# Modulation in half-width pieces of all row blocks from free tiles, and local attention with negated scores and the sink as a column

## The chip, the cores and the metric

The kernel runs on one core of a Trainium2 chip. The metric is device time in microseconds of one execution; a kernel's time is the median of its runs. The engines are TensorE (PE, its weight loads shown as PEld), VectorE (DVE), ScalarE (ACT), GpSimd (POOL) and SyncE (SP), which issues the kernel's DMAs.

## What is computed

Two layers of a diffusion backbone over 512 latent and 256 context tokens, model width 1024, in float32. Each layer is modulated by a projection of the conditioning, runs three attention branches beside each other and merges them:

```python
for l in range(DEPTH):
    mod_lat = silu_c @ w_mod[l] + b_mod[l]      # 1024 -> 3 * 1024: shift, scale, gate
    mod_ctx = silu_cc @ w_mod[l] + b_mod[l]
    ...
    x, ctx = hybrid_layer(x, ctx, mod_lat, mod_ctx, ..., l < DEPTH - 1)
return rms_norm(x, final_norm)

# one layer, cut
h_lat = rms_norm(x, norm_g) * (1.0 + scale) + shift
... = split_cols(h_lat @ w_in)                  # latent, differential and local attention, z, g
x = x + gate * merge_branches((ya_l, yb_l, yc_l), z_l, gm_l, w_branch, w_out)

# local attention: a window of 128 tokens on either side, all context tokens, and a sink logit per head
s_loc = where(mask, q @ k.T, NEG_INF);  s_ctx = q @ k_ctx.T        # q scaled by 64 ** -0.5
p = softmax(concatenate([sink, s_ctx, s_loc]));  o = p_ctx @ v_ctx + p_loc @ v_loc
```

The sink takes part in the maximum and in the sum of the softmax and has no value row.

## The kernel before

The program is written out ahead of time by a planner in Python (`Plan`), which keeps a clock of its own for each engine and for the DMA queue and puts the next piece that is ready by this clock into each engine's order. On the chip each engine then runs its order and waits on semaphores; where the planner's clock was wrong, an engine stands still at the head of its order. Two streams give PE its work. Stream A (`stream_a`) is attention: scores, then transposes and products with the values, for units of two rows of 128 queries, local attention first, then differential, then latent attention. Stream B (`stream_b`) is a list of entries: the projections in the order of `SEQ`, then the merges of the three branches in the order of `BR`, local attention's first, then the output projection. An entry may ask for a number of free tiles (`need`, with a reserve `keep`) and stands until they are there. Beside the streams, single pieces may be spawned with `P.pe`; a piece that is ready by the planner's clock goes ahead of both streams.

Weights come through `weight_stream`: SP loads each item of 512 KB into one of two buffers `ws`, ACT writes its high half into a tile `wh` and DVE its low half, and PE multiplies three passes (high-high, high-low, low-high). A `ws` buffer is free again when its item is `staged`, that is split; an item with `split=False` keeps its buffer until its entry has run. All other loads and stores also go through SP's one queue, in the planner's order. Activations live in 46 tiles of 128 x 768 (`slot`, `free`, `room`).

The modulation is a product of `sil` (the conditioning of both token groups, in 32 columns) with `w_mod`, a chunk `n` of 512 columns at a time, eight row blocks `kt` of 128. Block `kt` writes the 32 partitions of strip `kt % 4` of one bank, so two blocks add up in each strip, and `mod_fin` adds the four strips with another product. Chunks 0 to 3 of layer 0 are worked in the setup (`mod_load`, `mod_now`, not changed). Chunks 4 and 5 of layer 0 (its gate) and all six chunks of layer 1 are entries of stream B (`mod_entry`): four entries for each chunk, each with two row blocks of 512 columns as one unsplit item of the weight stream. Layer 0's eight stand ahead of its merges; layer 1's 24 follow one at a time after each `z` and `g` entry and every odd `b` entry of layer 0's merges (`some_mod`), until the list is empty. The planner charges a DMA 620 ns on SP's queue, then 650 ns, one ns for 350 bytes, and 1050 ns to land (`dma_t`).

Local attention's softmax (`soft_sink`, line 849) has for each row of 128 queries: one DVE scan that reads the scores from PSUM, adds the mask (0 or -1e30), writes them to a tile and takes the maximum, beginning with the sink (L858); a sign flip on DVE (L861); Exp of the sink on ACT into a column of its own; Exp of the scores on ACT with their sum; the sum of both on DVE; the reciprocal (L865); and the scaling by it, on DVE or ACT as the planner has it. There are 96 such rows in layer 0 and 64 in layer 1. L309, L323, L325, L330, L341 and L444 are helpers (ACT, DVE and POOL operations, the DMA and the matmul), so groups are told apart by their tiles; L579 is the modulation's matmul.

Of the kernel before, what the change touches and what calls it, by code (L numbers as in the profile page):

```python
# [18 lines left out]
AF = mybir.ActivationFunctionType  # L19
# [33 lines left out]
def shape_tables():  # L53

    pos = np.arange(LT)
    row, col = (pos // 64).astype(np.float32), (pos % 64).astype(np.float32)

    def ang(nf):
        inv = np.float32(10000.0) ** (-np.arange(nf, dtype=np.float32) / np.float32(nf))
        inv = inv.astype(np.float32)  # L60
        return np.concatenate([row[:, None] * inv, col[:, None] * inv], axis=1).astype(np.float32)

    a = ang(16).T
    p = np.arange(128)
    hd = a[p % 32]
    sgn = np.where(p % 64 < 32, -1.0, 1.0)[:, None]
    m = ang(8).T[p % 16]
    tab = np.concatenate([np.cos(hd), np.sin(hd) * sgn, np.cos(m), np.sin(m)], axis=1).astype(np.float32)
    ks = (np.sin(ang(8).T[np.arange(32) % 16]) * np.where(np.arange(32) < 16, -1.0, 1.0)[:, None])
    i, j = np.arange(128)[:, None], np.arange(128)[None, :]  # L70
    below = np.where(j >= i, 0.0, -1e30)
    above = np.where(j <= i, 0.0, -1e30)
    z = np.zeros((128, 128))
    mask = np.concatenate([below, z, above, z, z, below, z, z, z], axis=1)
    sel = np.zeros((128, 2))
    for g in range(4):
        sel[32 * g, 0] = sel[32 * g + 1, 1] = 1.0
    f = np.float32
    return {"tab": tab, "ktab": ks.astype(f), "mask": mask.astype(f), "sel": sel.astype(f)}
# [156 lines left out]
def hybrid_kernel(tc, x_in, c_in, ctx_in, c_ctx, w_mod, b_mod, norm_g, w_in, q_norm, w_uq, kv_norm, w_ukv,  # L236
# [52 lines left out]
    def tiny(n=1):  # L289
        return sb.tile([128, n], F32, name=nm("ti"), tag=f"ti{n}", bufs=24)  # L290
# [8 lines left out]
    def act(ready, out, in_, func=AF.Copy, scale=1.0, bias=None, accum=None, psum=True):  # L299
        kw = {}  # L300
        if accum is not None:
            kw["accum_out"] = accum
        if bias is not None:
            kw["bias"] = bias
        cost = 0.83 * fsz(out) + (51 if psum else 93) + (93 if accum is not None else 0)
        if not isinstance(scale, float) or bias is not None:
            cost += 93
        t = yield from P.on("A", ready, cost,
                            lambda: nc.scalar.activation(out=out, in_=in_, func=func, scale=scale, **kw))  # L309
        return t  # L310

    def dve(ready, emit, n, fast=False, ptr=False):
        t = yield from P.on("V", ready, (0.52 if fast else 1.04) * n + 70 + (60 if ptr else 0), emit)
        return t
# [25 lines left out]
    def dma(out, in_):  # L340
        nc.sync.dma_start(out=out, in_=in_)  # L341
        n = 4
        for s in out.shape:
            n *= s
        return dma_t(n)
# [39 lines left out]
    def item(load, parts=None, split=True, size=1024):  # L385

        done = When()
        return dict(load=load, parts=parts, split=split, size=size, ready=When(), done=done, staged=When() if split else done)
# [111 lines left out]
    def columns(st, n, t, out):  # L500
        o = {}

        def emit():
            o["p"], o["r"] = bk.take()
            nc.tensor.transpose(out=o["p"][:, 0:n], in_=st[0:n, 0:128], identity=ident[0:n, 0:n])
        t = yield from P.pe(lambda: max(t, bk.gate()), 110.0, emit)
        t = yield from dve(t, lambda: nc.vector.tensor_copy(out, o["p"][:, 0:n]), n)
        o["r"].t = t
        return t
# [35 lines left out]
    def setup2():  # L545

        st, v, pr = slot(), slot(), slot()
        n, t = rows_of(st, (q_norm[0], kv_norm[0], subln[0], b_mod[1], norm_g[1], q_norm[1], kv_norm[1], subln[1]))
        tv = 0.0
        for i, a in enumerate((lq1, lk1, lq2, lk2)):  # L550
            tv = max(tv, dma(v[:, i * 128:(i + 1) * 128], a.rearrange("l d -> (l d)").partition_broadcast(128)))
        dma(sinkt, sink.rearrange("l h -> (l h)").partition_broadcast(128))
        dma(rope, tab[:, 0:2 * LT].rearrange("p (a n) -> p a n", a=2))

        def chain():
            tcol = yield from columns(st, n, t, cols[:, 32:32 + n])
            vv = v[:, 0:512].rearrange("p (a l d) -> p a l d", a=4, l=2)
            prv = pr[:, 0:256].rearrange("p (m l d) -> p m l d", m=2, l=2)
            ta = tv
            for m in range(2):  # L560
                ta = yield from tt(ta, prv[:, m], vv[:, 2 * m], vv[:, 2 * m + 1], ALU.mult)
            d4, e4 = tiny(4), tiny(4)
            ta = yield from dve(ta, lambda: nc.vector.tensor_reduce(out=d4, in_=pr[:, 0:256].rearrange("p (a d) -> p a d", a=4), axis=AX.X, op=ALU.add), 256)
            ta = yield from act(ta, e4, d4, func=AF.Exp, psum=False)
            ta = yield from tt(ta, lamt, e4[:, 0:2], e4[:, 2:4], ALU.subtract)
            for l in range(2):
                li = 0.8 - 0.6 * math.exp(-0.3 * l)
                o = l * NCOL
                for t0, dst, src, k, op in ((ta, lamt[:, l:l + 1], lamt[:, l:l + 1], li, ALU.add),
                                            (tcol, subc[:, l:l + 1], cols[:, o + COL_SUB:o + COL_SUB + 1], li - 1.0, ALU.mult),  # L570
                                            (tcol, qnc[:, l], cols[:, o + COL_QN:o + COL_QN + 3], 96.0 ** -0.5, ALU.mult)):
                    yield from dve(t0, lambda: nc.vector.tensor_scalar(out=dst, in0=src, scalar1=k, scalar2=None, op0=op), 3)
            free(3)
        P.spawn(chain())


    def mod_mm(pm, kt, wv):
        g = kt % 4
        nc.tensor.matmul(pm[32 * g:32 * g + 32, :], lhsT=sil[:, kt], rhs=wv, start=kt < 4, stop=kt >= 4)  # L579

    def mod_fin(l, n, pm, rel, t):

# [264 lines left out]
        row["t"].t = t  # L847

    def soft_sink(u, row, p, rel, t):
        lo, hi = u["span"]  # L850
        n = hi - lo
        mx, nmx, s, e, r = tiny(), tiny(), tiny(), tiny(), tiny()
        sk = sinkt[:, u["l"] * 16 + row["h"]:u["l"] * 16 + row["h"] + 1]
        yield room(1)
        pt_ = slot()
        row["P"] = pt_
        mk = u["mask"]()
        t = yield from dve(t, lambda: nc.vector.tensor_tensor_reduce(  # L858
            out=pt_[:, 0:n], in0=p[:, lo:hi], in1=mk, scale=1.0, scalar=sk, op0=ALU.add, op1=ALU.max, accum_out=mx), n, ptr=True)
        rel.t = t  # L860
        t = yield from dve(t, lambda: nc.vector.tensor_scalar(out=nmx, in0=mx, scalar1=-1.0, scalar2=None, op0=ALU.mult), 1)  # L861
        t1 = yield from act(t, e, sk, func=AF.Exp, bias=nmx, psum=False)
        t = yield from act(t1, pt_[:, 0:n], pt_[:, 0:n], func=AF.Exp, bias=nmx, accum=s, psum=False)
        t = yield from tt(t, r, s, e, ALU.add)
        t = yield from dve(t, lambda: nc.vector.reciprocal(out=r, in_=r), 8)  # L865
        t = yield from normalise(t, pt_[:, 0:n], r)
        row["t"].t = t

# [417 lines left out]
    def build_layer(o):  # L1286
# [249 lines left out]
        def sec_sw():  # L1536
# [31 lines left out]
                    P.spawn(chain())  # L1568
            entry(sv_h, sv_its, need=6, keep=KEEP_SV)
            for pr in range(8):  # L1570
                qk_entry("sq", pr, C_SQ, 0.125, cx)
                if pr == 2:
                    qk_entry("sk", 1, C_SK, 1.0, True)

# [39 lines left out]
        m = [None] * 8  # L1614
        mH, mL, mt_ = [None] * 8, [None] * 8, [When() for _ in range(8)]
        o.m = {"HL": [mH, mL], "t": mt_}
        mod_left = [(n, j) for n in (2, 3, 0, 1, 4, 5) for j in range(4)]
        pm = {}

        def mod_entry(ll, n, j):  # L1620
            it = item(lambda t: [(t[:, 0:1024].rearrange("p (k c) -> p k c", k=2),
                                  w_mod[ll, j * 256:(j + 1) * 256, n * 512:(n + 1) * 512].rearrange("(k p) c -> p k c", p=128))], split=False)

            def h(it):
                yield lambda: max(at(it["ready"]), bk.gate() if j == 0 else 0.0)
                if j == 0:
                    pm["p"], pm["r"] = bk.take()
                for k in range(2):
                    mod_mm(pm["p"], 2 * j + k, it["ws"][:, k * 512:(k + 1) * 512])
                P.tick(550.0)  # L1630
                if j == 3:
                    P.spawn(mod_fin(ll, n, pm["p"], pm["r"], P.now + 200.0))
            entry(h, [it], need=0)

        def some_mod(k):
            for _ in range(k):
# [3 lines left out]
        if l == 0:  # L1640

            for n in (4, 5):
                for j in range(4):
                    mod_entry(0, n, j)

        def wide(it, X):
# [278 lines left out]
```

## Time and profile before

| | us |
|---|---|
| median of 3 runs | 2752.4 |
| lowest and highest run | 2744.74, 2753.49 |
| the profiled execution | 2746.83 |
| its span, first to last instruction | 2745.0 |
| PE busy in it | 2657.7 |
| DVE busy | 1655.3 |
| ACT busy | 1380.5 |
| POOL busy | 127.8 |
| mean granted clock of TensorE | 0.988 |

Times in the trace are microseconds from the span's start. A busy time is the union of an engine's instructions; matmuls are pipelined and their ends are modelled, so one matmul's record overlaps the next, and what a piece costs PE is read from its start to the start of the work after it. A value in square brackets in a timeline is the time that the engine stood idle ahead of the instruction, with what released it.

### The profile page before, as it was taken

The page shows a single profiled execution, that of the slowest core. Times are in us where ns is not written, and L with a number is a line of the kernel's source. Part 1 is how long each engine was busy: PE and PEld are TensorE (multiplying, and loading weights), DVE is VectorE, ACT ScalarE, POOL GpSimd, SP SyncE. Part 2 cuts the span into 40 slices and gives each one's busy share as a digit, 9 for nine tenths or more (in the row PEclk, how much of TensorE's full clock was granted, in tenths as well). Part 3 has the DMA queues.
Part 4 walks back from the last instruction along what each step waited for, and adds up shares of the span by engine and source line. Part 5 has one row for each costly group of instructions (what it writes and reads, how often), then busy time and mean ns, then how long its engine had stood idle before and what let it go on. Part 6 is the DMA issues. An engine that isn't in the chain of part 4 may idle for free.

```text
span 2745.0 us, 42932 instructions
## 1 busy us (share of the span) xinstructions
PE 2657.7 (97%) x16711; PEld 2308.7 (84%) x16711; DVE 1655.3 (60%) x3350; ACT 1380.5 (50%) x2860; POOL 127.8 (5%) x198
## 2 busy tenths in 40 slices
PE   7999999999999999999999999999999999999998
PEld 4888898888888878878888988898888789888888
DVE  4678778666676652133333578888767677634435
ACT  4667777555556442121222357877546555523332
POOL 0000000111100000000000000000011100000000
PEclk8999999999999999999999999999999999999999
DMA  6132211111122353353332443322112223443433
GB/s 228 45 92 83 73 42 46 49 51 48 44 68 87 107 187 105 93 175 93 91 86 62 139 125 92 105 57 67 40 48 55 58 68 102 127 136 110 123 101 130
DMA packets 328348, 249.58 MB, mean 91 GB/s; under 512 B 24548, under 2 KB 288320, under 8 KB 328144
## 3 DMA queue, kind: packets, MB, share of 16 engines
q1 hardware_dynamic: 328144, 246.83, 30.9%
q8 instruction: 131, 2.15, 0.3%
q14 instruction: 73, 0.60, 0.1%
HBM read 211.37 MB, written 35.41 MB: 90 GB/s over the span
## 4 chain that ended last, share of the span: by engine, by line
PE 78%; DVE 9%; ACT 7%; issue 3%; DMA 2%; POOL 1%; SPq 0%; DVEq 0%; ACTq 0%; POOLq 0%
PE wd L444 37%; PE bk L444 35%; PE bk L913 4%; ACT pt L309 3%; ACT s L309 3%; DVE pt L323 2%; DVE s L323 2%; PE bk L579 1%; DVE wh L323 1%; DVE s L858 1%; DVE s L330 1%; ACT wh L309 1%; DMA ws<-in_w_in_dram 1%; DVE ti L825 0%; POOL pt L325 0%
## 5 line engine op out<-in xcount | busy, mean ns | idle before, releaser
L444 PE MATMUL wd<-s,wh 128*128 128x512 f32 (+1 forms) x4392 | 855.5, 355 | 6.7 <-ACT wh L309 3.5
L444 PEld LDWEIGHTS wd<-s,wh 128*128 128x128 f32 x4392 | 725.7, 189 | 145.0 <-ACT s L309 12.9
L444 PE MATMUL bk<-s,wh 128*128 128x512 f32 (+1 forms) x3666 | 771.7, 356 | 18.4 <-DVE s L323 6.9
L444 PEld LDWEIGHTS bk<-s,wh 128*128 128x128 f32 x3666 | 582.5, 190 | 106.6 <-DVE s L323 9.8
L323 DVE TENSOR_TENSOR wh<-ws,wh 128x1024 fp32r<-128x1024 f32 (+4 forms) x294 | 325.1, 1112 | 343.1 <-ACT wh L309 341.4
L309 ACT ACTIVATE wh<-ws 128x1024 fp32r<-128x1024 f32 (+4 forms) x294 | 282.5, 967 | 297.1 <-PE wd L444 148.5
L309 ACT ACTIVATE pt<-bk 128x512 fp32r<-128x512 f32 (+3 forms) x604 | 341.4, 584 | 167.9 <-PE bk L913 102.8
L444 PE MATMUL bk<-wh,s 128*128 128x256 f32 x2688 | 352.9, 286 | 3.8 <-DVE wh L323 2.0
L444 PEld LDWEIGHTS bk<-wh,s 128*128 128x128 f32 x2688 | 333.3, 193 | 9.7 <-issue 3.2
L323 DVE TENSOR_TENSOR pt<-bk,pt 128x512 fp32r<-128x512 f32 (+3 forms) x400 | 257.6, 664 | 77.7 <-ACT pt L309 66.4
L444 PE MATMUL bk<-pt,s 128*128 128x256 f32 x1888 | 277.2, 288 | 13.3 <-DVE pt L323 10.2
L444 PEld LDWEIGHTS bk<-pt,s 128*128 128x128 f32 x1888 | 252.2, 191 | 38.8 <-DVE pt L323 16.7
L444 PE MATMUL wd<-s,s 128*128 128x256 f32 (+5 forms) x1872 | 275.9, 333 | 5.9 <-ACT s L309 5.5
L309 ACT ACTIVATE s<-wd,ti 128x768 f32<-128x768 f32 (+1 forms) x240 | 195.5, 818 | 140.8 <-DVE ti L825 78.5
L444 PEld LDWEIGHTS wd<-s,s 64*128 64x128 f32 (+2 forms) x1872 | 214.3, 191 | 36.7 <-ACT s L309 9.9
L913 PE MATMUL bk<-ident,s 128*128 128x128 f32 x1472 | 208.5, 275 | 9.8 <-DVE pt L323 2.4
L913 PEld LDWEIGHTS bk<-ident,s 128*128 128x128 f32 x1472 | 170.3, 142 | 35.9 <-ACT s L309 5.5
L309 ACT ACTIVATE s<-s,ti 128x512 f32<-128x512 f32 (+3 forms) x249 | 174.1, 708 | 15.0 <-DVE ti L865 8.1
L309 ACT ACTIVATE s<-bk 128x256 fp32r<-128x256 f32 (+5 forms) x291 | 113.6, 424 | 87.0 <-PE bk L444 85.0
L330 DVE SCALAR_TENSOR_TENSOR s<-s,wd 128x768 f32<-128x768 f32 (+1 forms) x58 | 47.6, 820 | 180.8 <-PE wd L444 108.1
L309 ACT ACTIVATE s<-wd 128x768 f32<-128x768 f32 (+1 forms) x58 | 40.9, 705 | 218.8 <-PE wd L444 218.8
L825 DVE TENSOR_REDUCE ti<-wd 128x1 f32<-128x768 f32 (+1 forms) x160 | 128.7, 843 | 18.2 <-PE wd L444 17.9
(98 smaller groups left out, 1734.6 us busy)
## 6 DMA issues: line engine op xcount, KB each, us to landing
ws<-in_w_in_dram SPq DMA_DIRECT2D x180, 512.0 KB
ws<-in_w_branch_dram SPq DMA_DIRECT2D x48, 512.0 KB
ws<-in_w_mod_dram SPq DMA_DIRECT2D x32, 512.0 KB
ws<-in_w_out_dram SPq DMA_DIRECT2D x24, 512.0 KB
y<-yo SPq DMA_DIRECT2D x80, 128.0 KB
s<-y SPq DMA_DIRECT2D x24, 384.0 KB
s<-s SPq DMA_DIRECT2D x22, 384.0 KB
s<-in_w_mod_dram SPq DMA_DIRECT2D x32, 256.0 KB
```

Of the source, the lines that this page charges most:

```text
L309: lambda: nc.scalar.activation(out=out, in_=in_, func=func, scale=scale, **kw))
L323: t = yield from dve(ready, lambda: nc.vector.tensor_tensor(out=out, in0=a, in1=b, op=op), n)
L330: t = yield from dve(ready, lambda: nc.vector.scalar_tensor_tensor(out=out, in0=a, scalar=s, in1=b, op0=op0, op1=op1), fsz(out), ptr=ptr)
L444: nc.tensor.matmul(o, lhsT=l, rhs=r, start=first, stop=last)
L579: nc.tensor.matmul(pm[32 * g:32 * g + 32, :], lhsT=sil[:, kt], rhs=wv, start=kt < 4, stop=kt >= 4)
L825: t = yield from dve(t, lambda: nc.vector.tensor_reduce(out=nmx, in_=p[:, lo:hi], axis=AX.X, op=ALU.max, negate=True), n)
L858: t = yield from dve(t, lambda: nc.vector.tensor_tensor_reduce(out=pt_[:, 0:n], in0=p[:, lo:hi], in1=mk, scale=1.0, scalar=sk, op0=ALU.add ...
L913: nc.tensor.transpose(out=pp[:, j * 256 + ri2 * 128:j * 256 + ri2 * 128 + 128], in_=row["P"][:, c:c + 128], identity=ident)
```

## The change

The modulation of layer 1 and of layer 0's gate no longer goes through the weight stream. An entry now covers all eight row blocks of 256 columns (two entries a chunk instead of four, so 16 in place of 32). It asks for three free tiles, loads 3, 3 and 2 row blocks of 256 columns into them with three DMAs, and spawns a piece with the eight products as soon as the loads have landed by the planner's clock; the entry itself returns at once. `some_mod` still adds one entry at a place, so layer 1's list is empty after 12 places.

In local attention the queries are scaled by -0.125, so the scores come out negated; the mask is 0 or +1e30, the sink is negated once in the setup, and the scan takes the minimum, which is the negated maximum. Exp gets the scale -1. The sink is copied into the column behind the scores by POOL, and Exp runs over one column more, so that its sum holds the sink.

```diff
-    below = np.where(j >= i, 0.0, -1e30)
-    above = np.where(j <= i, 0.0, -1e30)
+    below = np.where(j >= i, 0.0, 1e30)
+    above = np.where(j <= i, 0.0, 1e30)
...
-        dma(sinkt, sink.rearrange("l h -> (l h)").partition_broadcast(128))
+        ts = dma(sinkt, sink.rearrange("l h -> (l h)").partition_broadcast(128))
...
         def chain():
+            yield from dve(ts, lambda: nc.vector.tensor_scalar(out=sinkt, in0=sinkt, scalar1=-1.0, scalar2=None, op0=ALU.mult), 32)
...
-    def mod_mm(pm, kt, wv):
+    def mod_mm(pm, kt, wv, c=0):
         g = kt % 4
-        nc.tensor.matmul(pm[32 * g:32 * g + 32, :], lhsT=sil[:, kt], rhs=wv, start=kt < 4, stop=kt >= 4)
+        nc.tensor.matmul(pm[32 * g:32 * g + 32, c:c + fsz(wv)], lhsT=sil[:, kt], rhs=wv, start=kt < 4, stop=kt >= 4)
...
-        mx, nmx, s, e, r = tiny(), tiny(), tiny(), tiny(), tiny()
-        sk = sinkt[:, u["l"] * 16 + row["h"]:u["l"] * 16 + row["h"] + 1]
+        nmx, s, r = tiny(), tiny(), tiny()
+        h = u["l"] * 16 + row["h"]
+        sk = sinkt[:, h:h + 1]
...
+        yield from gps(0.0, lambda: nc.gpsimd.tensor_tensor(out=pt_[:, n:n + 1], in0=sk, in1=ones[:, 0:1], op=ALU.mult), 1)
         t = yield from dve(t, lambda: nc.vector.tensor_tensor_reduce(
-            out=pt_[:, 0:n], in0=p[:, lo:hi], in1=mk, scale=1.0, scalar=sk, op0=ALU.add, op1=ALU.max, accum_out=mx), n, ptr=True)
+            out=pt_[:, 0:n], in0=p[:, lo:hi], in1=mk, scale=1.0, scalar=sk, op0=ALU.add, op1=ALU.min, accum_out=nmx), n, ptr=True)
         rel.t = t
-        t = yield from dve(t, lambda: nc.vector.tensor_scalar(out=nmx, in0=mx, scalar1=-1.0, scalar2=None, op0=ALU.mult), 1)
-        t1 = yield from act(t, e, sk, func=AF.Exp, bias=nmx, psum=False)
-        t = yield from act(t1, pt_[:, 0:n], pt_[:, 0:n], func=AF.Exp, bias=nmx, accum=s, psum=False)
-        t = yield from tt(t, r, s, e, ALU.add)
-        t = yield from dve(t, lambda: nc.vector.reciprocal(out=r, in_=r), 8)
+        t = yield from act(t, pt_[:, 0:n + 1], pt_[:, 0:n + 1], func=AF.Exp, scale=-1.0, bias=nmx, accum=s, psum=False)
+        t = yield from dve(t, lambda: nc.vector.reciprocal(out=r, in_=s), 8)
...
-                qk_entry("sq", pr, C_SQ, 0.125, cx)
+                qk_entry("sq", pr, C_SQ, -0.125, cx)
...
-        mod_left = [(n, j) for n in (2, 3, 0, 1, 4, 5) for j in range(4)]
+        mod_left = [(n, j) for n in (2, 3, 0, 1, 4, 5) for j in range(2)]
         pm = {}

         def mod_entry(ll, n, j):
-            it = item(lambda t: [(t[:, 0:1024].rearrange("p (k c) -> p k c", k=2),
-                                  w_mod[ll, j * 256:(j + 1) * 256, n * 512:(n + 1) * 512].rearrange("(k p) c -> p k c", p=128))], split=False)
-
-            def h(it):
-                yield lambda: max(at(it["ready"]), bk.gate() if j == 0 else 0.0)
-                if j == 0:
-                    pm["p"], pm["r"] = bk.take()
-                for k in range(2):
-                    mod_mm(pm["p"], 2 * j + k, it["ws"][:, k * 512:(k + 1) * 512])
-                P.tick(550.0)
-                if j == 3:
-                    P.spawn(mod_fin(ll, n, pm["p"], pm["r"], P.now + 200.0))
-            entry(h, [it], need=0)
+            def h():
+                W = [slot() for _ in range(3)]
+                t = 0.0
+                for i, w in enumerate(W):
+                    k = min(3, 8 - 3 * i)
+                    t = max(t, dma(w[:, 0:k * 256].rearrange("p (k c) -> p k c", k=k),
+                                   w_mod[ll, 384 * i:384 * i + 128 * k, n * 512 + j * 256:n * 512 + j * 256 + 256].rearrange("(k p) c -> p k c", p=128)))
+
+                def chain():
+                    def emit():
+                        if j == 0:
+                            pm[n] = bk.take()
+                        for k in range(8):
+                            mod_mm(pm[n][0], k, W[k // 3][:, k % 3 * 256:k % 3 * 256 + 256], 256 * j)
+                    te = yield from P.pe(lambda: max(t, bk.gate() if j == 0 else 0.0), 750.0, emit)
+                    free(3)
+                    if j == 1:
+                        yield from mod_fin(ll, n, *pm[n], te)
+                P.spawn(chain())
+                return
+                yield
+            entry(h, need=3, keep=KEEP_U)
...
             for n in (4, 5):
-                for j in range(4):
+                for j in range(2):
                     mod_entry(0, n, j)
```

## Rows read from the trace of the kernel before

**Rows 1.** The page's busy times and shares of the span by engine, and its row of PE in 40 slices (tenths of busy time).

```profile
PE 2657.7 (97%) x16711; PEld 2308.7 (84%) x16711; DVE 1655.3 (60%) x3350; ACT 1380.5 (50%) x2860; POOL 127.8 (5%) x198
...
PE   7999999999999999999999999999999999999998
```

**Rows 2.** Busy times in stretches: the stretch, its length, then for each engine us busy and instructions, granted clock (1.00 is full), DMA share and GB/s. Local attention of layer 0 and layer 1, the first two merges of layer 0, a slice of 50 us in them, and the first 50 us.

```profile
100.00:450.00 350.00, 334.73 (x2196) 302.01 (x2194) 275.99 (x810) 261.76 (x631) 15.55 (x12) 0.98 0.24 66
1650.00:1910.00 260.00, 250.63 (x1566) 221.45 (x1564) 220.20 (x578) 203.62 (x448) 16.75 (x13) 1.00 0.30 79
990.00:1260.00 270.00, 264.03 (x1449) 211.16 (x1448) 80.77 (x89) 61.02 (x69) 0.00 (x0) 0.99 0.45 139
...
1150.00:1200.00 50.00, 46.95 (x256) 37.03 (x255) 21.47 (x24) 13.86 (x17) 0.00 (x0) 0.97 0.59 195
...
0.00:50.00 50.00, 32.75 (x146) 15.71 (x147) 17.78 (x58) 23.52 (x70) 4.76 (x12) 0.85 0.83 281
```

**Rows 3.** PE's timeline around entries of the modulation: start, us, engine, line, operation, out<-in, shape, count, and idle ahead with its releaser.

```profile
944.79 1.07 PE L579 MATMUL bk<-ws,sil 128*32 128x512 f32 x8
945.79 2.37 PE L444 MATMUL wd<-s,s 96*128 96x256 f32 x12
949.79 1.62 PE L579 MATMUL bk<-ws,sil 128*32 128x512 f32 x4 [1.64 <-DMA ws<-in_w_mod_dram]
...
962.73 1.07 PE L579 MATMUL bk<-ws,sil 128*32 128x512 f32 x8
...
968.62 1.46 PE L579 MATMUL bk<-ws,sil 128*32 128x512 f32 x8
...
1061.77 1.05 PE L579 MATMUL bk<-ws,sil 128*32 128x512 f32 x4
1062.75 8.62 PE L444 MATMUL wd<-s,wh 128*128 128x512 f32 x48
```

**Rows 4.** Busy time of the modulation's matmuls alone (line 579) in the two stretches that hold all 128 records that come from `ws`: stretch, length, PE and PEld busy and records, clock, DMA share, GB/s.

```profile
940.00:970.00 30.00, 6.18 (x32) 0.89 (x32) 0.94 0.47 152
990.00:1260.00 270.00, 25.25 (x96) 3.46 (x96) 0.99 0.45 139
```

**Rows 5.** PE's timeline: one chunk of layer 0's modulation in the setup, eight row blocks of 512 columns one after another (two of its records are missing in the trace), and a run of transposes.

```profile
33.06 1.99 PE L579 MATMUL bk<-s,sil 128*32 128x512 f32 x14
...
954.54 1.47 PE L913 MATMUL bk<-ident,s 128*128 128x128 f32 x12
```

**Rows 6.** SP's timeline (issues of DMAs), and the starts of ACT's weight splits that waited for such a load.

```profile
945.88 0.91 SPq L341 DMA_DIRECT2D ws<-in_w_mod_dram  x2
...
993.90 0.38 SPq L341 DMA_DIRECT2D ws<-in_w_mod_dram  x1
994.69 0.38 SPq L341 DMA_DIRECT2D ws<-in_w_in_dram  x1
...
1015.84 0.37 SPq L341 DMA_DIRECT2D ws<-in_w_in_dram  x1
...
1025.04 0.38 SPq L341 DMA_DIRECT2D ws<-in_w_in_dram  x1
...
1047.96 0.37 SPq L341 DMA_DIRECT2D ws<-in_w_branch_dram  x1
...
1021.01 1.06 ACT L309 ACTIVATE wh<-ws 128x1024 fp32r<-128x1024 f32 x1 [6.45 <-DMA ws<-in_w_in_dram]
...
1051.48 1.06 ACT L309 ACTIVATE wh<-ws 128x1024 fp32r<-128x1024 f32 x1 [4.81 <-DMA ws<-in_w_branch_dram]
```

**Rows 7.** PE's waits in 990 to 1260 (us in total, times, longest), and two rows of PE's timeline after such waits.

```profile
PE wd L444 <- ACT wh L309: 3.5, 3, 1.6
PE wd L444 <- DVE wh L323: 2.5, 3, 1.5
...
1015.87 8.15 PE L444 MATMUL wd<-s,wh 128*128 128x512 f32 x46 [0.53 <-DVE wh L323]
...
1189.60 9.48 PE L444 MATMUL wd<-s,wh 128*128 128x512 f32 x46 [1.45 <-DVE wh L323]
```

**Rows 8.** Groups of instructions by line over the whole span (count, busy us, mean ns of one, idle ahead and its releasers): the scan, the sign flip, the sum and the sink's Exp of local attention, and POOL's two-column product and rope product.

```profile
L858 DVE CUSTOM_DVE_ANT_0 s<-wd,s,sinkt 128x512 f32<-128x512 f32 (+2 forms) x160 | 116.8, 743 | 25.9 <-PE wd L444 25.3
...
L861 DVE TENSOR_SCALAR ti<-ti 128x1 f32<-128x1 f32 x160 | 21.6, 142 | 0.3
...
L323 DVE TENSOR_TENSOR ti<-ti,ti 128x1 f32<-128x1 f32 x160 | 24.6, 157 | 23.3 <-ACT s L309 22.1
...
L309 ACT ACTIVATE ti<-sinkt,ti 128x1 f32<-128x1 f32 x160 | 42.8, 289 | 16.6 <-DVE ti L861 16.0
...
L979 POOL TENSOR_TENSOR ti<-ti 128x2 f32<-128x2 f32 x40 | 8.8, 220 | 32.5 <-DVE ti L840 32.4
...
L325 POOL TENSOR_TENSOR pt<-pt,rope 128x512 f32<-128x512 f32 x52 | 67.1, 1290 | 764.3 <-ACT pt L309 595.5 <-PE bk L444 52.0 <-DVE ti L861 46.8
```

**Rows 9.** PE's waits in 98 to 450, local attention of layer 0.

```profile
PE bk L444 <- DVE pt L323: 8.2, 9, 2.1
...
PE bk L444 <- DVE ti L861: 1.4, 2, 0.9
```

**Rows 10.** PE's waits in 1650 to 1910, local attention of layer 1.

```profile
PE bk L444 <- DVE pt L323: 3.0, 6, 1.0
PE bk L444 <- DVE ti L861: 2.4, 3, 0.8
```

## The prediction

> **What bounds the kernel now.** I read the page's head first: TensorE (PE) is busy 97% of the span and in 38 of 40 slices nine tenths or more, while DVE has 60%, ACT 50% and POOL 5% [rows 1]. So an edit is worth what it takes off PE's own time, or off the stretches in which PE stands still; time saved on DVE or ACT counts only where PE waits for them. Then I read four stretches [rows 2]. Local attention of layer 0 (100 to 450) and of layer 1 (1650 to 1910) leave PE idle 15.3 of 350 and 9.4 of 260 us, with DVE at 79% and 85%: there DVE's order decides some waits. The first two merges of layer 0 (990 to 1260), in which layer 1's modulation is worked, leave PE 6.0 of 270 us, with DVE at 30%: there a wait is one for weights. The rest is bound by PE.
>
> **Part 1, the matmuls of the modulation.** A product of a 128-row block with `sil` makes two PE records and fills one strip of 32 columns of the array (`g = kt % 4`). In a single entry of before (two row blocks, 512 columns, 4 records) PE starts at 1061.77 and its next work at 1062.75: 0.98 us [rows 3]. Two entries one right after the other, with 8 records in all four strips, take 944.79 to 945.79, the same 1.00 us [rows 3]. So the strips run beside each other, and an entry that fills two of them pays for four. The 32 entries came in 29 visits: three rows of 8 records before 970, two of 4, then 24 of 4. Their busy time is 6.18 + 25.25 = 31.4 us [rows 4]; each record row of 1.05 overlaps the next work by 0.07, so on PE's path they cost 31.4 - 29 x 0.07 = 29.4 us.
>
> The new piece has all eight row blocks for 256 columns: 16 records, in four rounds over the four strips instead of two, each half as long. What a full round costs stands in the setup, where one chunk of eight blocks by 512 columns (four rounds, 14 of its 16 records kept) takes 1.99 us [rows 5]: about 0.2 of tail and 0.44 a round. Half the columns: 4 x 0.22 + 0.1 = 1.0 us. There are 16 pieces (12 for layer 1, 4 for layer 0's gate): 16 us. **Term: 16 - 29.4 = -13.4 us**, all on the path, since PE is bound here.
>
> The price that no row shows is how fast short records follow one another. The nearest row from above is 12 transposes of 128 columns in 1.47 us, 0.12 us each [rows 5]; at that pace 16 records take 1.96 us, 16 pieces 31.4 us, and the term is +2. I take the lower end, because a visit of 8 records in 1.00 us already shows more than one start per 0.12 us [rows 3] and the weight loads here are 32 columns, not 128. The range keeps -13.4 to +2. The Trainium skill (TensorE: Matmul & The Clock Gate, section "Wait — 56ns, not 53.3ns?") speaks against this choice: where the sequencer decodes in microcode each matmul costs about 62 ns, and if its weight load cost as much, 32 instructions would be an estimated 2.0 us a piece and the term again about +2; the visit of 8 records, 16 instructions in 1.00 us, fits that price too, so the trace doesn't exclude it. It is the third rival.
>
> **Part 2, the loads that move.** Before, each entry's 512 KB stood in one of the two `ws` buffers until its matmuls had run, so the weight behind it was asked for late: at 993.90 SP issues a modulation load and only at 994.69 the weight of the next product [rows 6]. In 990 to 1260 PE waits 3.5 us for ACT's and 2.5 us for DVE's half of a weight split [rows 7], and after the idle at 1189.60 46 matmuls take 9.48 us where the same 46 took 8.15 at 1015.87 [rows 7]: 1.3 us more, in a slice whose granted clock is 0.97 on the mean [rows 2], so part of it ran at 1.2 GHz and not at 2.4. That makes 7.3 us as the most this can return, and 0 the least. ACT's and DVE's own order holds part of it (their queues carry `u` work of the branch as well), so I take a good half. **Term: -4 us.**
>
> What is late next: the pieces bring three loads (384, 384, 256 KB) into free tiles, issued by SP when the entry comes up, and their matmuls are put into PE's order as soon as the planner believes them landed, 620 + 650 + 1 MB / 350 + 1050 ns = 5.3 us after the entry. If they land later, PE stands, and behind it everything in its order. A 512 KB weight takes 1015.84 to 1021.01 = 5.2 us from SP's issue to ACT's start, one of another tensor 1047.96 to 1051.48 = 3.5 [rows 6]. The setup moves 281 GB/s over its first 50 us [rows 2], so the second half megabyte adds 1.9 us: an estimate of 5.4 to 7.1 us against 5.3. The one such wait of before is 1.64 us, at 949.79, for a load of 945.88 [rows 3, 6]. In favour: a piece enters only between two groups of three matmuls, so on average later than its time, and SP, where nothing holds its queue, runs ahead of the plan by up to a weight's distance (1015.84 to 1025.04, 9.2 us [rows 6]). What is queued behind a blocked piece load on SP are the next `ws` loads, `s` and `y` of the branch and the `y` stores; two weights loaded ahead cover about 8.6 us each [rows 3]. I take 0.23 us a piece more than today: 16 x 0.23 = 3.6, less the 1.64 that goes. **Term: +2 us**, range -1.6 to +40 (2.5 us a piece, the first rival).
>
> **Part 3, local attention.** A row loses on DVE the sign flip (142 ns) and the sum (157 ns), on ACT the one-column Exp (289 ns) [rows 8]; 160 rows, so 47.8 us of DVE and 46.2 of ACT, and some 0.6 us of each row's chain. The scan itself (743 ns), Exp over one column more, reciprocal and scaling stay. POOL gains 160 one-column products; its two-column product took 220 ns [rows 8], so 35 us on an engine that is 95% idle. Hidden as long as a copy is done within DVE's 743 ns scan, which starts after it in the program; otherwise Exp waits on ACT, and behind it the splits `pt` that PE's products need. That cover fails where a rope product (1.29 us) stands ahead on POOL: some 25 POOL instructions fall into both stretches [rows 2], so even all of them exposed are 25 x 1.29 = 32 us of ACT, not of PE; I put 0 and keep +5 for the range.
>
> How much of DVE's relief reaches PE: at most its idle, 15.3 + 9.4 = 24.7 us. What DVE releases late is mainly the split `pt` (8.2 us in layer 0, 3.0 in layer 1) and directly the sign flip (1.4 and 2.4) [rows 9, 10]. DVE loses 47.8 of 496 busy us [rows 2], a tenth; the flip's waits go for the most part, a fifth to a third of the split's. **Term: -6 us**, range -20 to +5.
> The Trainium skill (SBUF — State Buffer, section "SBUF: two separate sides") says that GpSimd and a DVE instruction with two SBUF inputs exclude each other for a whole instruction. If each of 160 copies held DVE up for the 220 ns of the row, 35 of the 47.8 us would be lost and the term would be an estimated -1.6; no row here isolates such a wait, and the sum goes without it.
>
> **At nothing**: the negation of `sinkt` (one short DVE instruction, in a setup in which DVE works 17.8 of 50 us), mask constants, the scale's sign, the bank held between a chunk's two pieces (as four entries held it), three of 46 tiles for some 6 us a piece. If tiles were short, stream B would stand at the piece; the next entries of the branch ask for three tiles with the same reserve and would stand too.
>
> **Sum.** -13.4 - 4 + 2 - 6 = -21.4 us. The profiled execution took 2746.8 us (span 2745.0 and 1.8 around it); it would take 2725.4. It lies 5.6 under the median of the runs shown, so the median goes to 2752.4 - 21.4 = 2731.
>
> **Rivals.** *Late pieces (slower).* The planner's order puts a piece into PE's order at a planned landing. From 23.4 / 16 = 1.46 us of new wait a piece on, the gain is gone; at 2.5 us, half of what one 512 KB weight takes, it is +40 against -23.4, so 2769. For it: 949.79, and the 5.2 us for a half megabyte against 3.8 by the planner's sum [rows 6]. Against: SP's lead, and a DMA share of 0.45 in the stretch [rows 2]. 10%.
> *Given back.* Matmuls halve, weights bring 2, loads cost 8 (0.5 us a piece), attention nothing, since a new order of its pieces makes new waits: -13.4 - 2 + 8 = -7.4, so 2745. 20%.
> *No halving.* Short records set the pace: +2 - 4 + 2 - 6 = -6, so 2746. 8%.
> *Attention bound by DVE.* Most of its idle goes, and all of the weights': -13.4 - 7.3 + 2 - 20 = -38.7, so 2714. 10%.
>
> **How the numbers follow.** The forecast, 2731 with a range of its own of 2722 to 2741, has 52%. About 0.3%, 8.3 us, is what a measurement of this kernel can tell from no change: 2744.1 and 2760.7. Faster: the forecast but for a sliver (50%), the last rival (10%), 40% of the two in the middle (10%): 0.70. Same: 0.20. Slower: 0.10. For eight in ten I leave out half of the last rival below and the late pieces and a little more above: 2711 to 2752.
>
> **What would show it.** Right: L579 has 256 records near 16 us of busy time, visits of 16 records about 1.0 us from start to start, all before 1150; no `wh` waits of PE in the first merges; PE's `pt` waits in attention shorter, none on a sign flip. Wrong: PE rows at L579 with idle ahead of them until `s<-in_w_mod` lands, in most of 16 places; visits of 2 us; PE's idle in 100 to 450 as large as now, or POOL as a releaser of ACT.

## The result, and the profile after

The changed kernel takes 2719.4 us (4 runs, 2717.0 to 2721.1) against 2750.6 of before measured beside it: ratio 0.989, interval 0.987 to 0.991, so 31 us less. The forecast was 2731. The profiled execution took 2718.5 (span 2716.7), 28.3 less than the profiled execution of before, which lies 3.8 below the 2750.6.

To see where the time went I put the same weight's split on ACT (`wh<-ws`, which both kernels do 294 times in one order) beside each other. Start times on ACT's timeline, first of before, then of after, for splits 48, 72, 108, 144 and 228 (counted from 0):

```profile
566.11 1.04 ACT L309 ACTIVATE wh<-ws 128x1024 fp32r<-128x1024 f32 x1
894.35 0.42 ACT L309 ACTIVATE wh<-ws 128x256 fp32r<-128x256 f32 x1
1293.88 1.05 ACT L309 ACTIVATE wh<-ws 128x1024 fp32r<-128x1024 f32 x1
1575.23 1.06 ACT L309 ACTIVATE wh<-ws 128x1024 fp32r<-128x1024 f32 x1 [4.15 <-PE bk L444]
2339.61 1.06 ACT L309 ACTIVATE wh<-ws 128x1024 fp32r<-128x1024 f32 x1
```

```profile
560.82 1.04 ACT L309 ACTIVATE wh<-ws 128x1024 fp32r<-128x1024 f32 x1
888.94 0.42 ACT L309 ACTIVATE wh<-ws 128x256 fp32r<-128x256 f32 x1
1260.92 1.05 ACT L309 ACTIVATE wh<-ws 128x1024 fp32r<-128x1024 f32 x1
1542.28 1.06 ACT L309 ACTIVATE wh<-ws 128x1024 fp32r<-128x1024 f32 x1 [4.15 <-PE bk L444]
2311.08 1.05 ACT L309 ACTIVATE wh<-ws 128x1024 fp32r<-128x1024 f32 x1
```

Up to 561 the kernel is 5.3 us ahead (layer 0's projections and local attention), through differential attention nothing is added, by 1261 it is 33.0 ahead, through the third merge and the output nothing, and in layer 1's attention it loses 4.4. So 27.6 us were made between splits 72 and 108, the tail of latent attention and the first merges of layer 0. That stretch in both kernels (columns as in [rows 2]), before's first:

```profile
894.30:1293.90 399.60, 390.90 (x2250) 318.23 (x2250) 153.97 (x217) 116.44 (x191) 0.00 (x0) 0.99 0.42 128
```

```profile
888.90:1260.90 372.00, 371.18 (x2378) 317.18 (x2378) 150.54 (x213) 117.63 (x194) 0.00 (x0) 1.00 0.45 138
```

PE stood idle 8.7 us and now 0.8. Its timeline in the changed kernel, which answers to [rows 3]:

```profile
1006.82 1.07 PE L580 MATMUL bk<-s,sil 128*32 128x256 f32 x16
1007.82 8.61 PE L444 MATMUL wd<-s,wh 128*128 128x256 f32 x48
1016.36 1.07 PE L580 MATMUL bk<-s,sil 128*32 128x256 f32 x16
1017.36 1.34 PE L444 MATMUL wd<-s,wh 128*128 128x256 f32 x9
```

A piece of eight row blocks of 256 columns, 16 records, costs 1.00 us from start to start, what two row blocks of 512 columns cost before. The group of all 16 pieces has 17.8 us of busy time where [rows 4] has 31.4, and no idle ahead of it (busy, mean ns, idle):

```profile
L580 PE MATMUL bk<-s,sil 128*32 128x256 f32 x256 | 17.8, 385 | 0.0
```

Start to start, all visits sum to 16.4 us (17 visits, two of them one piece with another product in between). SP's timeline shows why no piece waits: its three loads go out right behind the weight ahead of them, and the piece that they serve starts at 1016.36, 11.4 us after the first issue.

```profile
1004.50 0.37 SPq L341 DMA_DIRECT2D ws<-in_w_in_dram  x1
1004.97 1.59 SPq L341 DMA_DIRECT2D s<-in_w_mod_dram  x3
```

PE's waits in 888.9 to 1260.9 are down to these two; none is for a weight (answers to [rows 7]):

```profile
PE bk L444 <- DVE pt L323: 0.5, 2, 0.3
PE wd L444 <- DVE s L330: 0.3, 1, 0.3
```

The clock had cost more than I read off one row. These stretches of before lie around waits of PE: it was busy 7.66 of 10 us and 6.55 of 9 us, and in the 4 us that follow the granted clock is 0.57, so part of them ran at 1.2 GHz; (1 - 0.57) x 4 = 1.7 us are lost each time. In the changed kernel the whole stretch, 888.9 to 1260.9, is at 1.00.

```profile
940.00:950.00 10.00, 7.66 (x55) 5.82 (x55) 7.19 (x14) 5.05 (x14) 0.00 (x0) 1.00 0.47 146
950.00:954.00 4.00, 4.00 (x14) 2.36 (x11) 1.11 (x3) 0.18 (x2) 0.00 (x0) 0.57 0.85 260
...
1180.00:1189.00 9.00, 6.55 (x39) 4.76 (x37) 6.94 (x8) 4.74 (x6) 0.00 (x0) 1.00 0.57 209
1189.00:1193.00 4.00, 3.40 (x9) 2.74 (x10) 3.09 (x4) 1.13 (x2) 0.00 (x0) 0.57 0.57 132
```

The 27.6 us are then: visits 29.4 to 16.4, 13.0; idle 7.9; clock 3.4; and 3.3 more. About 2 of these stand in the branch's products with weights (`wd<-s,wh`, 1540 records in both kernels): from start to start, without idle, they take 276.0 us before and 272.0 now, of which some 1.6 are the second fall of the clock. The record right ahead of a visit and the one right behind it take 0.54 us together where two others take 0.35, and 13 visits stand among these products where 24 did: a visit costs its neighbours some 0.19 us. About 1 us stays unexplained.

### The profile page after: what moved, and what is told of

It is laid out like the page before. It is cut to its first block, busy times and chain, and to the rows that moved or that the text cites. A ratio compares the mean times of both kernels' runs of the same rounds, so it can differ in the third digit from the quotient of the medians.

```text
span 2716.7 us, 43089 instructions
## 1 busy us (share of the span) xinstructions
PE 2635.6 (97%) x16839; PEld 2307.2 (85%) x16839; DVE 1620.5 (60%) x3033; ACT 1345.6 (50%) x2698; POOL 166.4 (6%) x358
## 4 chain that ended last, share of the span: by engine, by line
PE 80%; DVE 7%; ACT 5%; issue 4%; DMA 1%; POOL 1%; SPq 0%; DVEq 0%; POOLq 0%; ACTq 0%
PE wd L444 38%; PE bk L444 36%; PE bk L914 5%; ACT s L309 2%; ACT pt L309 2%; DVE pt L323 2%; DVE s L323 1%; DVE wh L323 1%; DVE s L330 1%; PE bk L580 1%; DVE s L862 1%; ACT wh L309 0%; DVE ti L826 0%; POOL pt L325 0%; PE bk L950 0%
## 5 line engine op out<-in xcount | busy, mean ns | idle before, releaser
L444 PE MATMUL bk<-s,wh 128*128 128x512 f32 (+1 forms) x3666 | 765.9, 355 | 18.6 <-DVE s L323 10.6
L309 ACT ACTIVATE s<-s,ti 128x513 f32<-128x513 f32 (+6 forms) x247 | 174.8, 716 | 16.3 <-DVE ti L862 11.1
L309 ACT ACTIVATE yo<-bk 128x256 f32<-128x256 f32 (+1 forms) x200 | 72.0, 382 | 149.2 <-PE bk L444 148.0
```

The costliest lines, as they stand in the source:

```text
L444: nc.tensor.matmul(o, lhsT=l, rhs=r, start=first, stop=last)
```

## The experiments

Each ran beside the kernel before, in five rounds; the first four beside 2749.2 us, the last four beside 2750.3.

**The modulation alone.** The diff without its attention half (mask, sink, `soft_sink`, the sign of the scale stay as before).

```diff
-        mod_left = [(n, j) for n in (2, 3, 0, 1, 4, 5) for j in range(4)]
+        mod_left = [(n, j) for n in (2, 3, 0, 1, 4, 5) for j in range(2)]
...
+            entry(h, need=3, keep=KEEP_U)
```

> The modulation's pieces alone, with local attention as before. My theory is that nearly the whole gain is made in layer 0's first merges by the modulation: 13 us of shorter matmuls and some 11 us of weight waits with the slow clock behind them. It expects 23 to 30 us less than before, so 2721 to 2728, and 256 records of 256 columns with about 18 us of busy time. The rival, that local attention carries a good part of what was gained, expects 20 us or less.

2721.0, ratio 0.9895 (0.9876 to 0.9913): 28 us less, nearly all of it. The whole change has 0.9889 (0.9869 to 0.9908), so what the attention half adds on top can't be told from nothing. Between splits 72 and 108 it takes 371.9 us, as the changed kernel does.

**Local attention alone.** The other half.

```diff
-        t1 = yield from act(t, e, sk, func=AF.Exp, bias=nmx, psum=False)
...
+        t = yield from act(t, pt_[:, 0:n + 1], pt_[:, 0:n + 1], func=AF.Exp, scale=-1.0, bias=nmx, accum=s, psum=False)
```

> Local attention's part alone, with the modulation in the weight stream as before. My theory expects 0 to 6 us less than before: layer 0's attention gains about 5, layer 1's gives about 4 of it back. The rival, that local attention is bound by VectorE and ScalarE and carries a good part, expects 8 us or more less.

2745.1, ratio 0.9984 (0.9973 to 0.9994): by the ratio 4.4 us less, with an interval from 1.6 to 7.4. Where the relief goes is seen at the last of layer 0's 96 scans on DVE, first in the profile of before, then after:

```profile
440.62 0.48 DVE L858 CUSTOM_DVE_ANT_0 s<-wd,s,sinkt 128x256 f32<-128x256 f32 x1
```

```profile
423.00 0.48 DVE L862 CUSTOM_DVE_ANT_0 s<-wd,s,sinkt 128x256 f32<-128x256 f32 x1
```

Stream A is 17.6 us ahead there, and 140 us later 5.3 are left: PE gave attention's products earlier and the projections' later, and gains little by that itself. Its waits for the split `pt` in 98 to 450 fall from 8.2 to 3.7 us and none is left on a sign flip [rows 9], but waits for `s` come up in their place (0.4 us for this line before), and its idle in 100 to 450 is 14.0 us against 15.3 [rows 2]:

```profile
PE bk L444 <- DVE pt L323: 3.7, 9, 0.8
PE bk L444 <- DVE s L330: 3.6, 2, 1.8
```

```profile
100.00:450.00 350.00, 336.02 (x2267) 303.92 (x2266) 271.35 (x648) 245.27 (x542) 37.07 (x107) 0.99 0.25 67
```

All four profiles with attention as before have 15.2 to 15.3 us there, the five with the new attention and GpSimd's copy 13.6 to 14.1. So 1.3 of the 4.4 us are PE's idle, and no row shows the rest. The 5.3 us of lead at split 48 are no measure of it: in the four profiles that split starts at 563.3 to 569.9, in the five at 560.8 to 564.2, on the mean 3.5 us apart, and up to there TensorE ran at 1.2 GHz for 37.5 us in the profile of before, 23.9 in the first of the changed kernel and 34.1 in the second.

The 4.4 us that layer 1's attention seemed to lose can't be put down to the change either. From split 144 to 228 the profile of before takes 764.4 us; the run above with before's attention, this one, and the changed kernel profiled again take 767.6, 768.7 and 767.9. The clock goes with it: TensorE was at 1.2 GHz for 10.2 us of that stretch in the profile of before and for 17.1 to 27.3 in the nine others. The first 160 us of it, in before and in the changed kernel, and the whole of it in the run with before's attention:

```profile
1575.00:1735.00 160.00, 149.96 (x980) 134.45 (x979) 122.90 (x290) 107.67 (x232) 11.42 (x12) 1.00 0.42 116
```

```profile
1542.00:1702.00 160.00, 150.91 (x955) 135.66 (x955) 115.33 (x249) 100.25 (x209) 18.11 (x32) 0.96 0.36 104
```

```profile
1547.30:2314.90 767.60, 746.99 (x4990) 662.24 (x4988) 579.18 (x1222) 491.54 (x1039) 57.18 (x82) 0.99 0.27 74
```

**All strips, inside the weight stream.** Attention as before; 32 entries of the weight stream as before, each with four row blocks of 256 columns.

```diff
+            cb, kh = j // 2 * 256, j % 2
...
-                for k in range(2):
-                    mod_mm(pm["p"], 2 * j + k, it["ws"][:, k * 512:(k + 1) * 512])
+                for k in range(4):
+                    mod_mm(pm["p"], 4 * kh + k, it["ws"][:, k * 256:(k + 1) * 256], cb)
```

> Local attention as before; the modulation stays in the weight stream with 32 entries and the same bytes, but an entry has four row blocks of 256 columns instead of two of 512, so all four strips of the array work in each visit. My theory expects visits of 0.5 to 0.6 us instead of 0.98, so 11 to 14 us less than before, while TensorE's waits for weight splits in the first merges stay near 6 us. The rival, that the gain is the freed weight stream and a shorter visit is hidden, expects at most 4 us less.

2740.4, ratio 0.9974 (0.9963 to 0.9985): by the ratio 7 us less (4 to 10; the medians lie 8.8 apart), under the 11 to 14 that I expected. The visits are as short as expected (1032.19 to 1032.76, 0.57 us), but PE's waits for weight splits grew from [rows 7]'s 6.0 to 7.6, its idle in the stretch from 8.7 to 11.0, and the clock fell three times instead of twice, which costs 5.1 us instead of 3.4 (0.94 on the mean of 1000 to 1050). PE's timeline, its waits in 891.5 to 1284.2, and two stretches:

```profile
1032.19 0.64 PE L579 MATMUL bk<-ws,sil 128*32 128x256 f32 x8
1032.76 8.62 PE L444 MATMUL wd<-s,wh 128*128 128x512 f32 x48
```

```profile
PE wd L444 <- ACT wh L309: 5.6, 3, 2.3
PE wd L444 <- DVE wh L323: 2.0, 2, 1.4
```

```profile
891.50:1284.20 392.70, 381.73 (x2379) 320.59 (x2378) 153.77 (x217) 115.84 (x191) 0.00 (x0) 0.99 0.43 131
...
1000.00:1050.00 50.00, 48.11 (x277) 39.88 (x277) 17.92 (x22) 13.15 (x15) 0.00 (x0) 0.94 0.48 144
```

So within the stream about 12 us of PE's time were saved (busy time of the group 31.5 to 19.8) and 4 to 5 given back, 2.3 as idle and 1.7 as clock among them: where a weight comes late, PE reaches it sooner and waits longer.

**Outside the stream, narrow visits.** Attention as before; two row blocks of 512 columns from two free tiles, two entries at each place.

```diff
+                W = [slot() for _ in range(2)]
...
+                        for i in range(2):
+                            mod_mm(pm[n][0], 2 * j + i, W[i][:, 0:512])
...
-                    some_mod(1)
+                    some_mod(2)
```

> Local attention as before; the modulation is loaded into free tiles outside the weight stream, two entries at each place, but an entry keeps its two row blocks of 512 columns, so a visit fills two strips. My theory expects 29 to 32 us of busy time of these matmuls as before, the waits for weight splits in the first merges gone with the slow clock after them, and 8 to 13 us less than before. The rival, that the weight waits only move elsewhere, expects at most 4 us less.

2744.6, ratio 0.9983 (0.9970 to 0.9997): 4.7 us less (0.8 to 8.2), again under what I expected. In 899.1 to 1292.2 PE's idle is 2.9 us with no wait for a weight, and the clock is full: the weights' half of the gain is there, 5.8 + 3.4 = 9.2 us. But the visits cost more than before, 34.2 us of busy time against 31.5, and 2.6 of that lie in one of the 30: two joined entries, 8 records, that take 4.29 us from start to start (952.22 to 956.51) where such a visit took 1.00 [rows 3]. Their loads came one after another, among 15 that SP issued from 949.35 to 958.22, and 1.6 us of waits for them count as idle. The stretch takes 393.1 us instead of 399.6.

```profile
952.22 2.65 PE L579 MATMUL bk<-s,sil 128*32 128x512 f32 x6 [0.91 <-DMA s<-in_w_mod_dram]
955.53 1.04 PE L579 MATMUL bk<-s,sil 128*32 128x512 f32 x2 [0.66 <-DMA s<-in_w_mod_dram]
```

```profile
899.10:1292.20 393.10, 390.19 (x2251) 314.15 (x2250) 152.69 (x217) 114.56 (x191) 0.00 (x0) 1.00 0.42 131
```

Together the two halves bring 6.9 + 6.5 us in this stretch, the whole 27.6. The halves don't add up: short visits need weights in time to be worth their 13, and weights in time bring 9 only if the loads that replace the stream don't cost visits.

**The changed kernel again.** No edit; the mark for the three runs beside it.

> The changed kernel unaltered, as the mark for the three runs beside it and for what two profiles of one program differ by. Expected: 2719 within 4 us; in its profile the stretch of layer 1's attention within 2 us of 768.8, the same stage of layer 0's attention 3 to 5 us off the first profile.

2718.6, ratio 0.9887 (0.9874 to 0.9900). In its profile split 48 is 3.5 us ahead of before where the first profile had 5.3, so the two lie 1.8 apart and not 3 to 5.

**Pieces believed early.**

```diff
-                    te = yield from P.pe(lambda: max(t, bk.gate() if j == 0 else 0.0), 750.0, emit)
+                    te = yield from P.pe(lambda: max(t - 5000.0, bk.gate() if j == 0 else 0.0), 750.0, emit)
```

> The changed kernel, but the planner believes a piece's loads landed 5 us sooner, so a piece stands in TensorE's order some 5 us earlier against its loads. It prices my rival of late pieces and the lead that SP's queue gives. In the changed kernel a piece starts 9 to 10 us after SP issued its first load and never waits. My theory: the lead covers 3 to 4 us of the 5, so most of the 16 pieces wait 1 to 2.5 us for their loads and the kernel loses 15 to 40 us against the changed one, mostly as waits on the modulation's loads with a slower clock here and there. The rival, that loads land so early that the lead is over 5 us everywhere, expects no change.

2739.8, ratio 0.9964 (0.9955 to 0.9974): 21 us more than the changed kernel beside it. Five of the 16 pieces now wait (I had expected most), the one at 1004.08 for loads that SP issued from 1000.62 to 1002.11, and the stretch from split 72 to 108 takes 386.4 us instead of 371.9. PE's waits in it and one piece:

```profile
PE bk L580 <- DMA s<-in_w_mod_dram: 7.7, 9, 2.7
```

```profile
1004.08 0.63 PE L580 MATMUL bk<-s,sil 128*32 128x256 f32 x6 [1.39 <-DMA s<-in_w_mod_dram]
1005.21 1.36 PE L580 MATMUL bk<-s,sil 128*32 128x256 f32 x10 [0.50 <-DMA s<-in_w_mod_dram]
```

So the rival of late pieces has the right mechanism, and its price of 2.5 us a piece fits the five that wait: of the 14.5 us lost in the stretch 1.7 are a fall of the clock, and the rest is 2.6 for each of the five, or 0.8 on the mean of 16. The other 6 to 7 of the 21 us lie where no piece stands, in stages whose profiles differ by as much. What kept the rival away is the lead of SP's queue, less than 5 us more than needed at the five pieces; the other eleven don't wait even so.

**Whole chunks.** Six tiles and six loads an entry, eight row blocks by 512 columns in one piece.

```diff
-                W = [slot() for _ in range(3)]
+                W = [slot() for _ in range(6)]
...
-            entry(h, need=3, keep=KEEP_U)
+            entry(h, need=6, keep=KEEP_U)
```

> The changed kernel with a piece for a whole chunk: eight row blocks by 512 columns from six free tiles, 8 pieces instead of 16, the same matmuls. If the visit to the modulation has a price of its own (the product ahead and the one behind don't overlap with it, 0.2 to 0.3 us a visit beside the four rounds), 8 visits fewer give 1 to 3 us. The rival, that six tiles held for each piece hold up the branch's own tiles, expects 3 to 15 us more.

2725.3, ratio 0.9909 (0.9896 to 0.9923): 6.7 us more than the changed kernel beside it, as the rival had it and not my 1 to 3 less. The visits are shorter: seven of the eight take 1.86 us where two pieces took 2.00 (the eighth, which waits for its loads, 3.71), and from the product ahead to the product behind all 8 take 18.6 us where 17 took 21.4. But PE waits in 890.3 to 1268.3 for the branch's own operands:

```profile
PE wd L444 <- ACT s L309: 3.3, 3, 1.8
PE wd L444 <- DVE s L330: 1.5, 1, 1.5
```

SP's timeline shows them behind six loads in its one queue:

```profile
955.82 7.88 SPq L341 DMA_DIRECT2D s<-in_w_mod_dram  x6
964.41 0.34 SPq L341 DMA_DIRECT2D s<-y  x1
965.18 0.34 SPq L341 DMA_DIRECT2D s<-s  x1
```

That the wait comes from this queue and not from the tiles held is argued from these rows, not tried apart.

**The sink's copy on VectorE.**

```diff
-        yield from gps(0.0, lambda: nc.gpsimd.tensor_tensor(out=pt_[:, n:n + 1], in0=sk, in1=ones[:, 0:1], op=ALU.mult), 1)
+        yield from dve(0.0, lambda: nc.vector.tensor_tensor(out=pt_[:, n:n + 1], in0=sk, in1=ones[:, 0:1], op=ALU.mult), 1)
```

> The changed kernel with the copy of the sink's column on VectorE instead of GpSimd: 160 instructions of some 0.15 us back on VectorE, none of GpSimd ahead of the Exp. My theory, that TensorE's own work bounds the attention stretches and VectorE's relief bought little, expects no change within 4 us. The rival, that GpSimd's copies hold up VectorE or ScalarE and eat the relief, expects 5 us or more less.

2721.8, ratio 0.9894 (0.9881 to 0.9907), 3 us more than the changed kernel beside it and within the two intervals: no change that could be told, so there is no sign that GpSimd's copies eat up the relief. No version tried beats the changed kernel; the modulation alone equals it within the intervals.

## Why the prediction was right, and which terms were off

The direction and the place were right; the size, 21.4 forecast and 31 measured, was low by a third. 2719.4 lies within 2711 to 2752, but under the forecast's own range of 2722 to 2741, and the weights' term, put third, came out second. By the prediction's own steps:

- *The matmuls, -13.4:* measured -13.0 (29.4 to 16.4), and some -2 more beside the visits, which the sum left out. The reading that a visit pays for four strips whatever it fills held, and a round of half the columns takes half the time (a visit of 0.57 us against 1.00). The third rival is out: 16 matmuls with their weight loads take 1.00 us a piece. The Trainium skill's 62 ns a matmul (TensorE: Matmul & The Clock Gate, section "Wait — 56ns, not 53.3ns?") would fit 16 of the 32 instructions, not all of them; the estimate of 2.0 us a piece doesn't hold here, and a whole chunk, 32 matmuls with their loads, takes 1.86 us, 58 ns a matmul and so less than 62.
- *The freed weight stream, -4, at most -7.3:* this is the term that was mis-sized. It brought 7.9 us of idle and 3.4 us of clock, 11.3 in all, above the bound, and the bound itself was wrong: I took the clock from one row (1.3 us), though the trace held two falls of 1.7, and of PE's idle only the waits in 990 to 1260. And I took half because I thought that ACT's and DVE's own order held the rest; the narrow run shows every weight wait gone with the stream freed. The clock's part isn't fixed either (see the last section).
- *The loads of the pieces, +2:* measured 0; nothing waits. The price was right in kind (14.5 us in the merges when the pieces stand 5 us earlier), and SP's lead, which I named in favour, settled it.
- *Local attention, -6:* measured -4.4 alone (1.6 to 7.4), and 2 to 3 on top of the modulation, which can't be told from nothing. The size may be luck: the step that part of PE's idle goes did not come out as reasoned. The waits named, on `pt` and the sign flip, fell as forecast, but others came in their place, and PE's idle in 100 to 450 went from 15.3 to 14.0 us only, close to the sign of being wrong that I had named. In layer 1's local attention (1650 to 1910 of before) it is 8.5 to 9.4 us in the four profiles with the old attention and 7.4 to 9.8 in the five with the new. Where the rest of the 4.4 comes from stays open. The relief was smaller too, 35 us of DVE's busy time (1655.3 to 1620.5) and 35 of ACT's instead of 47.8 and 46.2. The rival in which attention is bound by DVE is out; that its 2714 lies nearer to the result than 2731 is chance, since it put 20 us on attention and 7.3 on the weights. GpSimd's copies cost 271 ns each on the mean, not 220, and no wait is put down to them:

```profile
L861 POOL TENSOR_TENSOR s<-sinkt,ones 128x1 f32<-128x1 f32 x160 | 38.3, 271 | 69.8 <-PE bk L914 30.4 <-PE wd L444 14.8 <-DMA q<-s 10.6
...
L862 DVE CUSTOM_DVE_ANT_0 s<-wd,s,sinkt 128x512 f32<-128x512 f32 (+2 forms) x160 | 117.3, 743 | 46.9 <-PE wd L444 46.7
```

- That mean hides two prices. Of the 160 copies 134 take 189 ns on the mean and 26 take 347 to 1177, 695 on the mean; each of the 26 ends 45 to 53 ns after a VectorE instruction that reads tiles and no PSUM, such as `pt<-pt,pt`. First their shortest, median and longest time, then four copies on POOL, the second of which takes 676 ns, and DVE's instruction there:

```profile
L861 POOL TENSOR_TENSOR s<-sinkt,ones x160: 180/189/1177, 95.2 to 1859.2; 128x1 f32<-128x1 f32 x160
274.95 1.10 POOL L861 TENSOR_TENSOR s<-sinkt,ones 128x1 f32<-128x1 f32 x4
275.03 0.69 DVE L323 TENSOR_TENSOR pt<-pt,pt 128x512 f32<-128x512 f32 x1 [2.70 <-POOL pt L325]
```

  The Trainium skill (SBUF — State Buffer, section "SBUF: two separate sides") has GpSimd and a VectorE instruction with two SBUF inputs exclude each other for a whole instruction; the trace agrees, with GpSimd as the one that stands. VectorE was not held up as the estimate of -1.6 supposed: the 19 `pt<-pt,pt` beside a copy take 688 ns and the 39 others 689, and the scan 743 as before [rows 8]. With the copies on VectorE it is the other way round: five of them take 0.37 to 1.16 us, and each of these ends 9 to 16 ns after a rope product on GpSimd.
- The two halves of the modulation leave 14.2 of the 27.6 us to their combination. In these rows that is 4.7 of visits (busy time 31.5 to 17.8, where the halves have -11.7 and +2.7), 4.4 of idle (-7.9 against +2.3 and -5.8), 1.7 of clock (-3.4 against +1.7 and -3.4), and 3.4 in the other products.
- What stays open: some 1 of the 27.6 us in the merges, and where local attention's 4.4 us come from.

## What to carry to other kernels

Where matmuls fill only some strips of the array, lay a visit out so that it fills all of them: eight row blocks of 256 columns cost what two of 512 did. Count the stall of a late operand together with the slower clock after it, over the whole stage and not from one row, and take a load that sits long in a short ring of buffers out of that ring. Relief on an engine that is 80% busy can come to little: here 35 us on DVE and 35 on ACT brought 4, as other waits of PE took the place of those that went. And of a gain of 12 us on PE a third came back as waits and clock where the next operand wasn't there sooner as well.

## What the runs showed that I had not expected

PE's clock fell after stretches with 2.3 and 2.5 us of idle in 10 and 9, each time at a cost of 1.7 us of full clock. But the same idle can pass without a fall. In the run with attention alone the same waits leave PE 7.76 of 10 us busy (939.5 to 949.5) and the clock stays at 1.00; in the run with whole chunks it is 6.67 of 10, and the clock is 1.00 then and in the 4 us after:

```profile
960.00:970.00 10.00, 6.67 (x42) 4.97 (x41) 6.85 (x12) 6.26 (x13) 0.00 (x0) 1.00 1.06 307
970.00:974.00 4.00, 4.00 (x48) 2.84 (x47) 1.77 (x3) 0.99 (x3) 0.00 (x0) 1.00 0.93 296
```

So what a wait costs in clock can't be read off its length, and the time of an execution goes with the clock it got: the 28 executions of before beside the first four runs go from 2742.4 us at a mean granted clock of 0.989 to 2757.5 at 0.981. Two profiles of one program differ by 1.8 us at the same weight of layer 0, and the ten profiles of layer 1's stage go from 764.4 to 772.6 us, so a difference of a few us in a stage of two single profiles tells nothing by itself.
